# Attention bands in a written-out order on three engines, the second norm spread between two products, three sums moved to VectorE, and a strip of memory

## The chip, the cores and the metric

The kernel runs on one core of a Trainium2 chip. The metric is the device time of one execution, in microseconds (us); the kernel before took 2420.7 us (median of three). Five engines work side by side and meet through semaphores: TensorE (PE, matrix products and transposes into PSUM), VectorE (DVE), ScalarE (ACT), GpSimd (POOL) and SyncE (SP, which issues the DMAs).

## The reference

A two-layer encoder on 1024 tokens of width 1024, all in float32. Per layer: a modulated RMS norm, one input projection, three groups of attention heads side by side, a norm of each group's output, an output projection into the residual; then a second modulated RMS norm and a gated FFN of hidden width 2816.

```python
h = rms_norm(x, g_attn[l]) * (1 + sc_a) + sh_a
qa, ka, va, qb, kb, vb, qc, kc, vc = split_cols(h @ w_in[l], IN_SPLITS)
ya = neighborhood_attention(...)      # A: 4 heads, 2-D window of 8 x 16, relative bias
yb = sliding_window_attention(...)    # B: 6 heads, |i - j| <= 128, bias, sink logit
yc = axial_attention(...)             # C: 6 heads, dense, q/k norm and rotary
y = concatenate([rms_norm(ya, ga), rms_norm(yb, gb), rms_norm(yc, gc)])
x = x + gt_a * (y @ w_o[l])
h = rms_norm(x, g_ffn[l]) * (1 + sc_f) + sh_f
gate, up = split_cols(h @ w_gu[l], (FFN_HIDDEN, FFN_HIDDEN))
x = x + gt_f * ((silu(gate) * up) @ w_down[l])
```

For an A or B head only keys near the query count, so for each block of 128 queries the scores form a band of at most 384 keys.

## The kernel before

**Numbers.** Float32 operands are split into a high and a low part (`hi`, `lo`); a full product is three matmuls (`mm3`, line 202), in the attention's value product two. Splitting costs one ACT instruction (the high part) and one subtraction on DVE or POOL (the low part): `split_tile` (153) gives `whi` and `wlo` of a weight tile, `y_split` (1520) the two halves of the attention output as operand `qk`.

**Who sets the order.** Every instruction passes through the class `Engine` (37 to 61), so all rows of the profile name its line 49. A scheduler may reorder the instructions of an engine as their data allow. `pin` (92) turns that off for chosen engines: from then on each instruction is chained to the one issued before it on the same engine, so that the engine runs them in the order in which the program writes them, and one that waits holds up all behind it.

**The attention stream** (1580 to 1651). The 64 units of work are "pairs": two blocks of 128 queries of one head. Pairs 0 to 23 are C pairs (dense, 1024 keys), 24 to 39 A pairs and 40 to 63 B pairs; A and B pairs are the *bands* (class `Band`, 1384; `PairA` and `PairB` give the bias). One pass `n` of the loop at 1584 issues steps of several pairs, in two halves `i`: `turn` of pair n, `pv` of pair n-1, and `qk` of the pairs that begin, three (`AHEAD`) or, in the bands, five (`AHEAD_B`) ahead. Only POOL is pinned in this loop (1582). A band pair goes through these steps:

- `qk` (1395): four score matmuls on PE into PSUM (tiles `sA`, `sB`); per block one fused DVE instruction that adds the bias and takes the row minimum (a custom operation, tile `pr`); the exponential on ACT with its sum; then, through `unfinished`, `divide` (1149): a reciprocal on DVE and two scalings on POOL.
- `turn` (1422): four PE transposes into a PSUM tile `T`, an ACT copy to the high part and a DVE subtraction to the low part (both named `pt`); one or two further transposes of the band's edges, copied by ACT (odd pairs) or DVE (even pairs) to `edge`.
- `pv` (1450, through `products`, 1258): four matmuls and one or two of the edges (each of these shows as two in the trace) into the PSUM tile `pv`, which an even pair opens and the following odd pair fills.
- `combine` (1280), behind the odd pair: ACT copies one half of `pv` to `cmb`, DVE adds the halves into the output `y`.

PSUM holds two tiles of two banks for scores (`psS`), three for `T`, and a single one for `pv` (`psV`). The tile `T` also serves the statistics and spreadings below.

Written among the pairs are other tasks (1598 to 1650). `preload` loads the heads of later pairs. After each group of heads, `norm_sum` (1491) squares `y` on ACT, `stats` (1640) sums over partitions with 16 small matmuls (`ps_st`) and computes 1/sqrt by eleven small DVE operations (`inv_sqrt`, 427), and `norm_scale` (1502) spreads the result with four transposes (`ps_r`), an ACT copy and multiplications on POOL. At 55 and 59 `y_split` prepares the output projection, at 59 and 61 `split_tile` splits two tiles of w_o, at 61 to 64 `o_rows` (1539) does the projection's first matmuls (`ps_o`), and at 62 two more tiles of w_o are loaded and split on DVE. After the loop comes the rest of that projection.

**Gate/up** (1845 to 2020). The FFN products use seven products for eight, per column block `q`: even q is gate, odd q is up. For the first seven blocks (`EARLY`, loop at 1979) products 1 and 2 come ahead, while the rest of the normed input is still being made; `t2_part`, `t3_part` and `t4_part` make its sums on DVE and split them (`ht1` to `ht4`, `h22`). `norm` is the generator `rstd_rows` (458): its first step is the statistic, its second the spreading of the second norm with four transposes (`ps_r`), taken as `rows` at line 1990, after block 1's products and the loading of further columns. In the second loop (2002) the other products follow. `gu_product` (1847) copies a product from PSUM on ACT (`u`, `sg`), adds on DVE, and has POOL do the sum of product 7 (1886) and the products of gate and up (1869, 2009).

**Memory.** The pool `ct` (830) lives in the projections of each layer; the five lines above `bias_rows` (959), where two tiles are allocated, run in layer 0 only, and a tile that is allocated there moves the addresses of what is allocated behind it.

## Time and profile before

| what | value |
|---|---|
| median of three runs | 2420.7 us (2420.62 to 2425.7) |
| the profiled execution's own time | 2422.97 us |
| its span in the profile | 2421.1 us |
| mean granted clock of PE | 0.994 |
| PE busy | 2350.5 us, 97% |
| DVE busy | 1766.8 us, 73% |
| ACT busy | 1194.3 us, 49% |
| POOL busy | 753.4 us, 31% |

The rows of the profile name a line, an engine, an operation and its tiles, as output, an arrow, and inputs. A group ends with its busy time, the mean of one instruction in ns, and the idle time of the engine just before these instructions with what ended it. A timeline row begins with its start and its duration. Successive matmuls overlap, so their durations add up to more than the time that they take; the distance between starts is the cost.

### The profile page before, as it was taken

The page shows a single profiled execution, that of the slowest core. Times are in us where ns is not written, and L with a number is a line of the kernel's source. Part 1 is how long each engine was busy: PE and PEld are TensorE (multiplying, and loading weights), DVE is VectorE, ACT ScalarE, POOL GpSimd, SP SyncE. Part 2 cuts the span into 40 slices and gives each one's busy share as a digit, 9 for nine tenths or more (in the row PEclk, how much of TensorE's full clock was granted, in tenths as well). Part 3 has the DMA queues.
Part 4 walks back from the last instruction along what each step waited for, and adds up shares of the span by engine and source line. Part 5 has one row for each costly group of instructions (what it writes and reads, how often), then busy time and mean ns, then how long its engine had stood idle before and what let it go on. Part 6 is the DMA issues. An engine that isn't in the chain of part 4 may idle for free.

```text
span 2421.1 us, 33439 instructions
## 1 busy us (share of the span) xinstructions
PE 2350.5 (97%) x11733; PEld 1955.2 (81%) x11733; DVE 1766.8 (73%) x2782; ACT 1194.3 (49%) x2250; POOL 753.4 (31%) x725
## 2 busy tenths in 40 slices
PE   8999999999999999999999999999999999999998
PEld 5778798888787887888787879987878888888886
DVE  5756898976958888586677579988787545447865
ACT  3421788954543333344543148897454333334443
POOL 1530345610344344300036114464005444430001
PEclk9999999999999999999999999999999999999999
DMA  8478215154245454586434851142524332329643
GB/s 263 149 237 274 62 27 145 47 193 138 87 145 178 157 189 147 176 268 195 148 93 120 283 178 27 45 140 70 194 93 153 125 100 96 114 92 304 209 129 109
DMA packets 305335, 356.95 MB, mean 147 GB/s; under 512 B 51964, under 2 KB 221788, under 8 KB 305168
## 3 DMA queue, kind: packets, MB, share of 16 engines
q1 hardware_dynamic: 283296, 342.07, 44.4%
q10 hardware_dynamic: 21504, 12.59, 2.0%
q8 instruction: 92, 1.51, 0.2%
q14 instruction: 75, 0.61, 0.1%
q0 software_dynamic: 368, 0.17, 0.0%
HBM read 269.79 MB, written 88.63 MB: 148 GB/s over the span
## 4 chain that ended last, share of the span: by engine, by line
PE 48%; DVE 4%; issue 4%; DMA 2%; ACT 2%; POOL 2%; ACTq 0%; SPq 0%; POOLq 0%; DVEq 0%
PE ps_w L49 21%; PE ps_d L49 14%; PE ps_o L49 3%; PE pv L49 2%; PE T L49 2%; PE ps_v L49 2%; PE sC L49 2%; DMA qkd<-qko 1%; ACT pr L49 1%; PE ps_c L49 1%; POOL ct L49 1%; PE ps_ab L49 0%; DVE acc L49 0%; DMA graw<-gpd 0%; POOL pr L49 0%
## 5 line engine op out<-in xcount | busy, mean ns | idle before, releaser
L49 PE MATMUL ps_d<-wpt 128*128 128x512 f32 x1848 | 424.3, 390 | 2.4 <-ACT wpt L49 2.1
L49 PEld LDWEIGHTS ps_d<-wpt 128*128 128x128 f32 x1848 | 345.5, 188 | 76.4 <-issue 3.0
L49 POOL TENSOR_SCALAR pr<-pr,rs 128x1024 f32<-128x1024 f32 (+2 forms) x248 | 187.0, 768 | 227.8 <-DVE rs L49 212.8
L49 POOL TENSOR_TENSOR sg<-sg,u 128x512 f32<-128x512 f32 x86 | 125.5, 1461 | 354.5 <-ACT sg L49 117.9
L49 PE MATMUL pv<-pt,vs 128*128 128x256 f32 x1088 | 181.4, 297 | 7.3 <-ACT pt L49 2.7
L49 ACT CAST wpt<-w 128x512 fp32r<-128x512 f32 x154 | 95.7, 621 | 185.8 <-PE ps_d L49 168.0
L49 DVE TENSOR_TENSOR pt<-T,pt 128x512 fp32r<-128x512 f32 x272 | 178.5, 682 | 8.5 <-ACT pt L49 7.1
L49 PE MATMUL T<-identr,pr 128*128 128x128 f32 x1176 | 175.6, 273 | 2.6 <-ACT edge L49 0.8
L49 ACT CAST pt<-T 128x512 fp32r<-128x512 f32 x272 | 153.1, 586 | 40.5 <-PE T L49 38.1
L49 ACT COPY u<-ps_w 128x512 f32<-128x512 f32 x128 | 75.1, 586 | 192.1 <-PE ps_w L49 192.0
L49 DVE TENSOR_TENSOR wpt<-w,wpt 128x512 fp32r<-128x512 f32 x154 | 108.9, 707 | 82.1 <-ACT wpt L49 82.1
L49 POOL TENSOR_TENSOR wpt<-ws,wpt 128x512 fp32r<-128x512 f32 x80 | 111.6, 1395 | 180.8 <-ACT wpt L49 133.9
L49 PEld LDWEIGHTS pv<-pt,vs 128*128 128x128 f32 x1088 | 143.9, 189 | 21.1 <-DVE y L49 11.1
L49 PEld LDWEIGHTS T<-identr,pr 128*128 128x128 f32 x1176 | 139.9, 140 | 19.7 <-ACT edge L49 2.2
L49 DVE SCALAR_TENSOR_TENSOR acc<-wmt,condT,acc 128x512 f32<-128x512 f32 (+1 forms) x98 | 119.2, 1225 | 47.8 <-DMA wmt<-in_w_mod_dram 47.2
L49 ACT CAST wpt<-ws 128x512 fp32r<-128x512 f32 x176 | 107.8, 622 | 61.4 <-issue 26.6
L49 DVE TENSOR_TENSOR wpt<-ws,wpt 128x512 fp32r<-128x512 f32 x96 | 81.6, 861 | 60.3 <-ACT wpt L49 60.2
L49 DVE TENSOR_TENSOR wpt<-graw,wpt 128x512 fp32r<-128x512 f32 x154 | 110.0, 715 | 19.0 <-ACT wpt L49 19.0
L49 DVE TENSOR_REDUCE rs<-sC 128x1 f32<-128x1024 f32 x88 | 107.3, 1221 | 16.4 <-PE sC L49 12.4
L49 DVE TENSOR_TENSOR ws<-wr 128x512 f32<-128x512 f32 x88 | 80.0, 911 | 51.3 <-POOL wpt L49 48.1
L49 ACT CAST wpt<-graw 128x512 fp32r<-128x512 f32 x154 | 95.0, 617 | 43.3 <-DMA graw<-gpd 37.9
L49 PE MATMUL ps_w<-h22h,wpt 128*128 128x512 f32 x352 | 111.2, 397 | 4.6 <-ACT sg L49 3.6
(298 smaller groups left out, 5964.4 us busy)
## 6 DMA issues: line engine op xcount, KB each, us to landing
wr<-in_w_gu_dram SPq DMA_DIRECT2D x92, 512.0 KB, 4.1
gpd<-sg SPq DMA_DIRECT2D x154, 256.0 KB, 4.4
graw<-gpd SPq DMA_DIRECT2D x76, 512.0 KB, 3.6
w<-in_w_down_dram SPq DMA_DIRECT2D x110, 256.0 KB, 5.4
wmt<-in_w_mod_dram SPq DMA_DIRECT2D x48, 512.0 KB, 6.4
qk<-qkd SPq DMA_DIRECT2D x44, 512.0 KB, 6.8
wst<-in_w_o_dram SPq DMA_DIRECT2D x32, 512.0 KB, 3.7
wmt<-in_w_mod_dram SPq DMA_DIRECT2D x64, 256.0 KB, 3.8
```

The costliest lines, as they stand in the source:

```text
L49: ins = op(*args, **kwargs)
```

## The change

Four things change.

1. **Bands.** The methods of `Band` are cut into steps: `scores` (PE and DVE), `exps` (ACT), `divide` (DVE and POOL), `turn` (PE, the high copy and the edge copy), `low` (the DVE subtraction), `pv` (both halves), `fold` (the ACT copy `cmb`) and `combine` (the DVE addition). From pass 24 (`NC`) on PE, ACT, DVE and POOL are pinned, and one pass writes: low of n-1, addition of n-3, scores of n+4, exponentials of n+3, turn of n, pv and fold of n-2, division of n+2; then the tasks above, in their old places. `AHEAD_B` is 4, the loop runs two passes longer, and the norms' squares follow the additions, two passes later.
2. **The second norm's spreading** stands between the two early products of block 1.
3. **Three POOL operations go to DVE**: product 7's sum for blocks 0 and 1, and the product of gate and up at the head of block 1.
4. **A strip** of 192 bytes a partition is allocated in layer 0's `ct`.

```diff
--- before.py
+++ after.py
@@ -955,6 +955,7 @@
             sp.dma_start(mB, C["maskB"])
             dve.tensor_copy(t5h[:, 0, :], t5)
             dve.tensor_tensor(out=t5h[:, 1, :], in0=t5, in1=f32(t5h[:, 0, :]), op=ALU.subtract)
+            pad(ct, 48)
 
         def bias_rows():
 
@@ -1274,18 +1275,24 @@
                             stop=(n == len(movs) - 1 and i == len(mvs) - 1),
                             skip_group_check=True,
                         )
-                if part and self.p % 2:
-                    self.combine()
-
-            def combine(self):
-
+
+            def fold(self):
+
+                if self.p % 2 == 0:
+                    return
                 r0 = (self.row % 2) * 64
                 o0 = 64 - r0
+                self.t = atp.tile([P, H], F32, name="cmb", tag="cmb", bufs=1)
+                act.copy(self.t[r0 : r0 + 64], self.pvt[o0 : o0 + 64])
+
+            def combine(self):
+
+                if self.p % 2 == 0:
+                    return
+                r0 = (self.row % 2) * 64
                 half = self.p // 2
-                t = atp.tile([P, H], F32, name="cmb", tag="cmb", bufs=1)
-                act.copy(t[r0 : r0 + 64], self.pvt[o0 : o0 + 64])
                 to = y[r0 : r0 + 64, self.row // 2, :]
-                a, b = self.pvt[r0 : r0 + 64], t[r0 : r0 + 64]
+                a, b = self.pvt[r0 : r0 + 64], self.t[r0 : r0 + 64]
                 if self.by_columns:
                     to = to.rearrange("p (r j i) -> p j r i", j=8, i=8)
                     to = to[:, half * 4 : half * 4 + 4]
@@ -1343,6 +1350,9 @@
                     ],
                     part,
                 )
+                if part:
+                    self.fold()
+                    self.combine()
 
         def load_q(dst, oc, j):
             sp.dma_start(f32(dst), qkd[oc, j].rearrange("z p t -> (z p) t"))
@@ -1392,62 +1402,60 @@
                 self.pr = self.flat[:, 0:770].rearrange("p (c k) -> p c k", c=2)
                 self.spans = [(0 if p > 0 else P, 384), (0, 384 if p < 3 else 256)]
 
-            def qk(self, c):
+            def scores(self):
                 rs, p, sk = self.rs, self.p, self.sk
-                if c == 0:
-                    self.s = psS.tile([P, 2, 512], F32, name=self.name, tag="S")
-                s, pr = self.s, self.pr
-                j = 2 * p + c
-                a, b = self.spans[c]
-                for i in range(2):
-                    pe.matmul(
-                        s[:, c, a:b], self.q[:, j * P : (j + 1) * P],
-                        self.k[i][:, (j - 1) * P + a : (j - 1) * P + b],
-                        start=(i == 0), stop=(i == 1),
+                s, pr = psS.tile([P, 2, 512], F32, name=self.name, tag="S"), self.pr
+                for c, (a, b) in enumerate(self.spans):
+                    j = 2 * p + c
+                    for i in range(2):
+                        pe.matmul(
+                            s[:, c, a:b], self.q[:, j * P : (j + 1) * P],
+                            self.k[i][:, (j - 1) * P + a : (j - 1) * P + b],
+                            start=(i == 0), stop=(i == 1),
+                        )
+                    sv, pw, z = s[:, c, a:b], pr[:, c, a:b], self.bias(j, a, b)
+                    if z.ndim > 2:
+                        sv, pw = (t.rearrange("p (b k) -> p b k", k=P) for t in (sv, pw))
+                    dve.tensor_tensor_reduce(
+                        out=pw, in0=sv, in1=z, scale=1.0, scalar=BIG if sk is None else sk,
+                        op0=ALU.add, op1=ALU.min, accum_out=rs[:, c : c + 1],
                     )
-                sv, pw, z = s[:, c, a:b], pr[:, c, a:b], self.bias(j, a, b)
-                if z.ndim > 2:
-                    sv, pw = (t.rearrange("p (b k) -> p b k", k=P) for t in (sv, pw))
-                dve.tensor_tensor_reduce(
-                    out=pw, in0=sv, in1=z, scale=1.0, scalar=BIG if sk is None else sk,
-                    op0=ALU.add, op1=ALU.min, accum_out=rs[:, c : c + 1],
+
+            def exps(self):
+                for c, (a, b) in enumerate(self.spans):
+                    e = self.pr[:, c, a : b + (self.sk is not None)]
+                    act.activation(
+                        e, e, AF.Exp, bias=self.rs[:, c : c + 1], scale=-1.0,
+                        accum_out=self.rs[:, 2 + c : 3 + c],
+                    )
+
+            def divide(self):
+                divide([self.pr[:, c, a:b] for c, (a, b) in enumerate(self.spans)], self.rs)
+
+            def turn(self):
+                pr = self.pr
+                T, self.pt = t_tile(), [pt_tile() for _ in range(2)]
+                for b in range(2):
+                    for i in range(2):
+                        pe.transpose(
+                            T[:, 2 * b + i, :], pr[:, b, (1 - b + i) * P : (2 - b + i) * P], ident
+                        )
+                edges = [pr[:, 0, 0:P]] * self.left + [pr[:, 1, 2 * P : 3 * P]] * self.right
+                E = t_tile()
+                for i, src in enumerate(edges):
+                    pe.transpose(E[:, i, :], src, ident)
+                hi, lo = (
+                    t[:, 0:2, :].rearrange("p i (c q) -> p c i q", c=2) for t in self.pt
                 )
-                e = pr[:, c, a : b + (sk is not None)]
-                act.activation(
-                    e, e, AF.Exp, bias=rs[:, c : c + 1], scale=-1.0,
-                    accum_out=rs[:, 2 + c : 3 + c],
+                T = T.rearrange("p (c i) q -> p c i q", c=2)
+                act.copy(hi, T)
+                e = self.e = atp.tile([P, 2, P], F32, name="edge", tag="edge", bufs=3)
+                (act.copy if self.p % 2 else dve.tensor_copy)(
+                    e[:, 0 : len(edges)], E[:, 0 : len(edges)]
                 )
-                self.finish(pr[:, c, a:b])
-
...
+                self.low = lambda: sub(lo, T, f32(hi))
+
+            def pv(self):
                 k0, e = 2 * self.p, self.e
                 movs = [
                     (k0 + i, slice(0, 2 * P), [t[:, i, :] for t in self.pt]) for i in range(2)
@@ -1456,7 +1464,8 @@
                     movs.append((k0 - 1, slice(0, P), [e[:, 0]]))
                 if self.right:
                     movs.append((k0 + 2, slice(P, 2 * P), [e[:, int(self.left)]]))
-                self.products(movs, part)
+                for part in range(2):
+                    self.products(movs, part)
 
 
         class PairA(Band):
@@ -1578,22 +1587,52 @@
         later = {}
         N = len(stream)
         pairs = {}
-        AHEAD, AHEAD_B = 3, 5
+        AHEAD, AHEAD_B, NC = 3, 4, 24
         pin((pool,), True)
         made, done = 0, len(first_pairs)
-        for n in range(-AHEAD - 1, N + 1):
-            ahead = AHEAD if n + AHEAD < 24 else AHEAD_B
+        scored, worked = [], []
+        for n in range(-AHEAD - 1, N + 3):
+            ahead = AHEAD if n + AHEAD < NC else AHEAD_B
             begin = range(done, min(n + ahead + 1, N))
-            for i in range(2):
-                if 0 <= n < N:
-                    pairs[n].turn(i)
-                while unfinished:
-                    unfinished.pop(0)()
-                if 0 <= n - 1 < N:
-                    pairs[n - 1].pv(i)
-                for m in begin:
-                    if m < made:
-                        pairs[m].qk(i)
+            if n == NC:
+                pin((pe, act, dve), True)
+            if n < NC:
+                for i in range(2):
+                    if 0 <= n:
+                        pairs[n].turn(i)
+                    while unfinished:
+                        unfinished.pop(0)()
+                    if 0 <= n - 1:
+                        pairs[n - 1].pv(i)
+                    for m in begin:
+                        if m < min(made, NC):
+                            pairs[m].qk(i)
+                fresh = [pairs[m] for m in begin if NC <= m < made]
+                for b in fresh:
+                    b.scores()
+                    b.exps()
+                    b.divide()
+            else:
+                if NC <= n - 1 < N:
+                    pairs[n - 1].low()
+                if NC <= n - 3:
+                    pairs[n - 3].combine()
+                fresh = [pairs[m] for m in begin if m < made]
+                for b in fresh:
+                    b.scores()
+                for b in scored:
+                    b.exps()
+                if n < N:
+                    pairs[n].turn()
+                if NC <= n - 2 < N:
+                    pairs[n - 2].pv()
+                    pairs[n - 2].fold()
+                elif n == NC:
+                    for i in range(2):
+                        pairs[n - 1].pv(i)
+                for b in worked:
+                    b.divide()
+                scored, worked = fresh, scored
             done = max(done, min(begin.stop, made))
             while made < min(N, n + ahead + 2):
                 for key, make in preload.get(made, []):
@@ -1623,9 +1662,9 @@
                 o_rows(1, w01[1], range(NS)[2 * (n - 63) : 2 * (n - 62)])
             if n == 62:
                 wq = [w_rows(w_o, k * P, eng=dve) for k in korder[2:4]]
-            m = n - 1
+            m = n - 1 if n <= NC else n - 3
             for end, (chunks, width) in norms.items():
-                if begins[end] <= m <= end and (m - begins[end]) % 8 == 7:
+                if begins[end] <= m <= end and (m - begins[end]) % 8 == 7 and (n <= NC or m >= NC):
                     i = (m - begins[end]) // 8
                     if end not in gss:
                         gss[end] = gss_tile()
@@ -1648,7 +1687,7 @@
                             later.setdefault(n + 8, []).append(scale)
 
                         later.setdefault(n + 5, []).append(stats)
-        pin((pool,), False)
+        pin((pe, act, dve, pool), False)
         close(psV_cm)
         close(psT_cm)
         close(vs_cm)
@@ -1883,7 +1922,7 @@
             elif num == 7:
                 take("x")
                 t22 = t["22"]
-                pool.tensor_tensor(out=t22, in0=t22, in1=t["x"], op=ALU.add)
+                (pool if q > 1 else dve).tensor_tensor(out=t22, in0=t22, in1=t["x"], op=ALU.add)
                 done(o[:, hi], t["22"], pool)
             elif num == 3:
                 add("12")
@@ -1980,14 +2019,14 @@
             for i in range(2):
                 a = [w[:, 4 * i : 4 * i + 4] for w in early[q]]
                 gu_product(q, PRODUCTS[i], a)
+                if q == 1 and i == 0:
+                    rows = next(norm)
             if q + 4 < EARLY:
                 early.append(first_cols((q + 4) % 2 * FF + (q + 4) // 2 * 2 * P))
             elif raw0 is None:
                 raw0 = gu_raw(0)
             if q == 0:
                 next(norm)
-            if q == 1:
-                rows = next(norm)
             if 1 <= q < 5:
                 bs.append(t2_part(q - 1, rows))
             if q == 1:
@@ -2006,7 +2045,9 @@
                 up = q % 2
                 e = sg[q // 2][0][:, 0:H]
                 if up:
-                    pool.tensor_tensor(out=e, in0=e, in1=quads[q]["11"], op=ALU.mult)
+                    (pool if q > 1 else dve).tensor_tensor(
+                        out=e, in0=e, in1=quads[q]["11"], op=ALU.mult
+                    )
             for i, p in enumerate(PRODUCTS[2 if q < EARLY else 0 :]):
                 gu_product(q, p, ahead.get())
                 if i == 1 and q < EARLY and not up:
```

More of the change, by code (lines that the diff above doesn't have):

```diff
@@ L1422, in turn @@
-            def turn(self, c):
-                pr = self.pr
-                T = t_tile()
-                if c == 0:
-                    self.pt = [pt_tile() for _ in range(2)]
-                    for b in range(2):
-                        for i in range(2):
-                            pe.transpose(
-                                T[:, 2 * b + i, :], pr[:, b, (1 - b + i) * P : (2 - b + i) * P],
-                                ident,
-                            )
-                    hv, lv = (
-                        t[:, 0:2, :].rearrange("p i (c q) -> p c i q", c=2) for t in self.pt
-                    )
-                    split_pt(T.rearrange("p (c i) q -> p c i q", c=2), hv, lv)
-                    return
-                e = self.e = atp.tile([P, 2, P], F32, name="edge", tag="edge", bufs=3)
-                n = 0
-                for left, here in ((True, self.left), (False, self.right)):
-                    if here:
-                        src = pr[:, 0, 0:P] if left else pr[:, 1, 2 * P : 3 * P]
-                        pe.transpose(T[:, n, :], src, ident)
-                        n += 1
-                if self.p % 2:
-                    act.copy(e[:, 0:n], T[:, 0:n])
-                else:
-                    dve.tensor_copy(e[:, 0:n], T[:, 0:n])
@@ L1450, in pv @@
-            def pv(self, part):
+                s, pr = psS.tile([P, 2, 512], F32, name=self.name, tag="S"), self.pr
[13 more added lines that the diff above has]
+                        op0=ALU.add, op1=ALU.min, accum_out=rs[:, c : c + 1],
+                    )
```

1 line of the change is left out of this document (removed).

## The prediction

> **What bounds the kernel now.** The page's first part comes first: TensorE (PE) is busy for nearly the whole span, so time moves only where PE is idle, slow or given other work.
>
> ```profile
> span 2421.1 us, 33439 instructions
> PE 2350.5 (97%) x11733; PEld 1955.2 (81%) x11733; DVE 1766.8 (73%) x2782; ACT 1194.3 (49%) x2250; POOL 753.4 (31%) x725
> ```
>
> A busy share can hide pipelined matmuls, so I next asked for the stretches that the change touches: the bands of layer 0 (from the first transpose of pair 24 to the last matmul of pair 63), the same of layer 1, two parts of layer 0's bands (split at the first transposes of pairs 28 and 57), gate/up of layer 0, and a short piece of that. Columns: bounds and length, busy time of each engine (count), granted clock, DMA share, GB/s.
>
> ```profile
> core 0: us, PE busy (x) PEld busy (x) DVE busy (x) ACT busy (x) POOL busy (x), PEclk, DMA share, GB/s
> 389.90:498.20 108.30, 103.19 (x733) 90.26 (x731) 97.91 (x292) 96.13 (x248) 66.73 (x117) 1.00 0.36 103
> 1570.50:1678.85 108.35, 103.36 (x734) 90.49 (x733) 98.18 (x292) 96.22 (x248) 66.93 (x118) 1.00 0.36 103
> 398.23:475.87 77.64, 74.43 (x535) 65.16 (x534) 69.05 (x228) 71.22 (x194) 52.29 (x95) 1.00 0.36 104
> 475.87:498.46 22.59, 20.69 (x135) 17.33 (x134) 21.51 (x41) 17.43 (x36) 8.95 (x13) 1.00 0.23 75
> 596.00:640.00 44.00, 40.42 (x170) 32.27 (x169) 43.72 (x64) 23.20 (x39) 5.11 (x3) 0.96 0.22 72
> 636.50:640.00 3.50, 3.46 (x9) 2.79 (x10) 3.38 (x5) 1.25 (x2) 1.71 (x1) 0.58 0.87 293
> ```
>
> In the bands three engines are near full at once: VectorE (DVE) 90%, ScalarE (ACT) 89%, PE 95%. No single one sets the pace; their order does. In gate/up DVE is full (43.72 of 44.00), PE waits for it, and at 636.5 PE's clock fell to 0.58.
>
> The groups of the bands (busy, mean ns, idle before) and a short timeline give what one pair costs.
>
> ```profile
> L49 PE MATMUL T<-identr,pr 128*128 128x128 f32 x220 | 37.7, 274 | 1.3 <-ACT edge L49 0.4 <-DVE edge L49 0.3 <-DVE pt L49 0.2
> L49 PE MATMUL pv<-pt,vs 128*128 128x256 f32 x176 | 34.2, 306 | 1.7 <-DVE y L49 0.8 <-DVE pt L49 0.5
> L49 DVE TENSOR_TENSOR pt<-T,pt 128x512 fp32r<-128x512 f32 x42 | 28.8, 687 | 1.3 <-ACT pt L49 0.8
> L49 ACT CAST pt<-T 128x512 fp32r<-128x512 f32 x41 | 23.9, 584 | 3.4 <-PE T L49 3.0
> L49 ACT ACTIVATE pr<-pr,rs 128x385 f32<-128x385 f32 x36 | 22.1, 615 | 0.6 <-POOL pr L49 0.4
> L49 PE MATMUL pv<-edge,vs 128*128 128x128 f32 x120 | 20.2, 274 | 0.0
> L49 DVE TENSOR_TENSOR y<-pv,cmb 64x512 f32<-64x512 f32 x20 | 13.7, 686 | 1.5 <-ACT cmb L49 1.1
> L49 ACT COPY cmb<-pv 64x512 f32<-64x512 f32 x20 | 11.6, 581 | 2.5 <-PE pv L49 2.1
> L49 DVE TENSOR_TENSOR wlo<-wst,whi 128x1024 fp32r<-128x1024 f32 x5 | 6.8, 1369 | 0.3 <-ACT whi L49 0.2
> L49 ACT CAST whi<-wst 128x1024 fp32r<-128x1024 f32 x5 | 5.2, 1048 | 0.7 <-DMA wst<-in_w_o_dram 0.7
> L49 ACT ACTIVATE gsq<-y 128x512 f32<-128x512 f32 x7 | 4.4, 635 | 0.6 <-DVE y L49 0.6
> L49 ACT ACTIVATE qk<-y,vecs 128x512 fp32r<-128x512 f32 x5 | 3.6, 726 | 0.0
> ```
>
> ```profile
> 440.25 0.52 PE L49 MATMUL pv<-pt,vs 128*128 128x256 f32 x3
> 442.56 0.60 PE L49 MATMUL T<-identr,pr 128*128 128x128 f32 x4
> 442.93 0.98 PE L49 MATMUL sB<-qk 128*128 128x384 f32 x4
> 443.97 1.84 PE L49 MATMUL ps_st<-onesr,gss 128*128 128x1 f32 x16
> ```
>
> ```profile
> 442.25 0.62 DVE L49 CUSTOM_DVE_ANT_0 pr<-sB,bz,sinkc 128x384 f32<-128x384 f32 x1
> 442.79 0.68 DVE L49 TENSOR_TENSOR pt<-T,pt 128x512 fp32r<-128x512 f32 x1
> 444.65 0.68 DVE L49 TENSOR_TENSOR y<-pv,cmb 64x512 f32<-64x512 f32 x1 [0.33 <-ACT cmb L49]
> ```
>
> Back to back, an instruction costs less than its duration. Four transposes last 0.60 and one 0.27, so they start (0.60-0.27)/3 = 0.11 apart; by the same reckoning a pv matmul of 256 columns costs 0.12, a score matmul of 384 columns about 0.18, and a transpose-sized edge matmul 0.11. On DVE the score step at 442.25 is followed 0.54 later, against its 0.62. One band pair on PE is thus: scores about 0.65, on average 5.5 transposes 0.60, pv 4 x 0.12 + 3 x 0.11 = 0.80; sum **2.05 us**. DVE, with the same overlap: two score steps 1.08, the low half 0.61, half a y addition 0.3, and some 0.15 for the small rest; sum about 2.1. ACT: two exponentials 1.2, the high half 0.50, half a cmb copy 0.25, the rest 0.15; sum about 2.1. The middle part now takes 77.64/29 = 2.68 us a pair, extras included.
>
> **The change, part by part.**
>
> *Bands, steady pace.* Nothing is computed less; the order is fixed and the steps stand further apart. A new limit is the one pv bank (psV). Between the pv of an odd pair and of the next even one stand the cmb copy (0.58) on ACT, the y addition (0.69) on DVE, the matmul's tail (about 0.16) and handoffs of about 0.04 each (three): 1.55. PE has the next scores and transposes for that time: 0.65 + 0.60 = 1.25. So 0.30 is lost each second pair, 0.15 a pair. For the passing to and fro between PE's three T banks and the copies I add 0.07: 2.05 + 0.15 + 0.07 = **2.27 us**, an estimate; its bounds are 2.05 (PE alone) and today's 2.68.
>
> *What is now nailed into that order.* Four kinds of work stood free before, and the engines could pass them; now all behind them wait. Each statistics step (pairs 29 and 47) is 16 small matmuls, 16 x 0.11 = 1.8 on PE, and DVE's chain of eleven small operations waits for them, with the next low half, y addition and score steps queued behind; I take 3.0 (bounds 1.8, PE's part alone, and 3.2, with two waiting DVE operations of 0.69). Each spreading (32, 50): four transposes 0.44 and ACT's copy ahead of its exponentials; I take 1.2 (0.44 to 1.5). The split of y at 55: ACT 0.73, then DVE about 0.7 (half of a wlo, which is twice as wide), and behind it the addition of pair 53 for which the pv of pair 54 waits; with handoffs I take 1.9 (bounds 0 and 2.3). Middle part: 29 x 2.27 + 2 x 3.0 + 2 x 1.2 + 1.9 = 76.1 against 77.64: **-1.5**.
>
> *The end of the bands.* At 59 a y split and a w_o split are written between the fold of pair 57 and its addition. After pv 57 ends there follow, in order: cmb 0.58, square 0.63, y 0.73, whi 1.05 (ACT), wlo 1.37, low half 0.69, addition 0.69 (DVE): 5.7, with handoffs 5.9; PE has only the transposes of pair 60 (0.60). I take 4.9 of idle time before pv 58, since the square may come earlier. At 61 the same without square and y: 0.58 + 1.05 + 1.37 + 0.69 + 0.69 = 4.4, with handoffs 4.7, against 0.60 of transposes and six output matmuls of 0.23 (1.4): 2.7; I take 2.3. At 62 two further weight rows are split, and their load stands between:
>
> ```profile
> wst<-in_w_o_dram SPq DMA_DIRECT2D x32, 512.0 KB, 3.7
> 594.97 0.39 PE L49 MATMUL ps_w<-h21l,whi 128*128 128x512 f32 x1
> 595.20 0.60 PE L49 MATMUL ps_r<-identr,rstd 128*128 128x128 f32 x4
> ```
>
> (The second and third rows also give a 512-column matmul: 0.23.) The load's 3.7 less the 2.0 that PE has meanwhile (transposes 0.60, output matmuls 1.4) leaves 1.7; I take 1.8 (0 to 3.7) before pv 62, whose opening waits for the addition of pair 61 behind that split. SyncE's queue stays unpinned, and the loads keep their place in the program. PE's work from transpose 57 to pv 63: 2 scores 1.3, 7 turns 4.2, 9 pv 7.2, 24 output matmuls 5.4: 18.1. With 4.9 + 2.3 + 1.8 it is 27.1 against 22.59 now: **+4.5** (bounds 18.1 and 29).
>
> *The start of the bands.* Pairs 24 to 27 run into the pinned order over pv 23, a dense one: I take +0.6 on the 8.33 us (398.23 less 389.90) to pair 28 (0 to +1.0). The scores of pair 28 move behind the first transposes: 0.65 earlier there, 0.65 later here, nothing in sum. POOL was pinned before; its two scalings per pair and the sink copies only move with the division, which stands two pairs (4.5 us) ahead of its transposes, and POOL is busy 66.73 of 108.30, 1.7 a pair: I cost this at nothing, and at up to 0.3 a pair if that lead is gone. The squares for the norms move two turns later with the additions that they read; they are the same instructions.
>
> *Clock.* PE's clock is the second price of an idle spell:
>
> ```profile
> 636.54 1.22 PE L49 MATMUL ps_w<-h22h,wpt 128*128 128x512 f32 x2 [1.80 <-ACT sg L49]
> 1298.62 0.50 PE L49 MATMUL ps_ab<-hh,wlo 128*128 128x512 f32 x1 [1.66 <-POOL wlo L49]
> 1298.70:1302.00 3.30, 3.30 (x15) 2.73 (x16) 3.27 (x6) 0.43 (x1) 3.22 (x4) 1.00 0.51 159
> ```
>
> After 1.80 idle the clock was 0.58 for 3.5 us; after 1.66 it stayed 1.00. So three of the new gaps (4.9, 2.3, 1.8) lie where a slow spell may come. One costs up to 3.5 x 0.42 = 1.5; as PE has slack here I take **+1.9** for the three (0 to 4.5). For T banks handed out in turn, where a slow reader holds up a free one, I take **+0.5** (0 to 3.8, one T copy of 0.58 for each of six to seven held turns).
>
> Bands, sum: 0.6 - 1.5 + 4.5 + 1.9 + 0.5 = **+6.0 a layer, +12.0**.
>
> By the Trainium skill, "TensorE: Matmul & The Clock Gate", section "What's actually happening", the clock halves after at least one idle window of some 3.4 us. By that rule only the 4.9 gap pays; the trace disagrees as far as it goes (1.80 was enough once), and I weigh it as a rival.
>
> *Gate/up.*
>
> ```profile
> 595.47 0.69 DVE L49 TENSOR_TENSOR u<-u,ps_w 128x512 f32<-128x512 f32 x1 [4.29 <-PE ps_w L49]
> 629.35 0.73 PE L49 MATMUL ps_w<-ht3h,wpt 128*128 128x512 f32 x2 [0.81 <-ACT sg L49]
> 633.32 0.73 PE L49 MATMUL ps_w<-ht4h,wpt 128*128 128x512 f32 x2 [0.96 <-ACT u L49]
> 631.79 1.77 DVE L49 TENSOR_TENSOR ht4l<-xb,ht4h 128x512 fp32r<-128x512 f32 x1
> 635.19 0.68 DVE L49 TENSOR_TENSOR ht4l<-xb,ht4h 128x512 fp32r<-128x512 f32 x1
> 631.32 3.40 POOL L49 TENSOR_TENSOR sg<-sg,u 128x512 f32<-128x512 f32 x2 [114.15 <-DMA wr<-in_w_gu_dram]
> ```
>
> DVE stands idle for 4.29 us before its full stretch, because the four spreading transposes (595.20) come after both products. Between the products they come 12 x 0.23 = 2.7 earlier. How much of it DVE gets depends on whether the addition of the second product, which ends where it did, stays ahead of the first norm operation: 0.5 if so, 2.7 if not. Three sums on DVE add 3 x 0.61 = 1.8; but while POOL did two of them, DVE's ht4l took 1.77 against 0.68 undisturbed, about 1.0 more for each sum: net -1.2. So DVE arrives 1.7 to 3.9 earlier where PE now waits 0.81 + 0.96 + 1.80 = 3.57, and with less than 1.8 idle the slow spell (1.5) can go. I take the middle for the waits and two fifths of the spell: 2.8 + 0.6 = **-3.4 a layer** (-1.0 to -5.1), **-6.8** in all.
>
> *The strip* has no instruction; it moves addresses in layer 0. No row shows an address at work: 0, bounds -2 and +2 (about the 1.66 us wait seen in that kind of stage).
>
> **Sum.** +12.0 - 6.8 = +5.2 on the profiled execution's own 2422.97 us (span 2421.1) is 2428.2. That execution lies 2.27 above the median of three, 2420.7; on the median the forecast is **2425.9 us**.
>
> **The rivals.**
>
> *Faster: the splits hide.* If ACT runs a pair ahead of PE, whi and y are done before pv 57 ends, and the end chain is only cmb, low half and addition (2.0 against 0.6 of turns). Then the end loses half of today's 4.5: 18.1 + 2.3 = 20.4 (-2.2), the split at 55 nothing (middle -3.4), no slow clock: 0.6 - 3.4 - 2.2 + 0.2 = -4.8 a layer; with gate/up 2420.7 - 9.6 - 6.8 = **2404.3**. For it: ACT is 11% idle. Against: its 2.1 a pair nearly equals the pace, so it gains no lead. It decides from about 3 us of ACT lead at pair 57.
>
> *Much slower: more slow clock, held T banks.* Four spells at 1.4 (the gap before pv 54 included) and 1.4 for banks in place of 1.9 and 0.5: 3.6 + 5.6 + 1.4 = 10.6 a layer; 2420.7 + 21.2 - 6.8 = **2435.1**. For it: 1.80 us sufficed at 636.54. Against: 1.66 did not at 1298.62.
>
> *No change: short gaps leave the clock alone.* Only the gap of 4.9 slows it (0.6): 3.6 + 0.6 + 0.5 = 4.7 a layer; +9.4 - 6.8 gives **2423.3**. The 1298.62 row speaks for it. That is also what the page's rule would give.
>
> **How the numbers follow.** About 0.2% (4.8 us) is what can be told from no change. The forecast (chance 0.45; 2413 to 2433) splits into 0.07 faster, 0.14 same, 0.24 slower. The faster rival has 0.20, all faster; the much slower one 0.17, all slower; the third 0.18: 0.04 faster, 0.12 same, 0.02 slower. Sums: faster 0.31, same 0.26, slower 0.43. The range runs from 2406 (half of the faster rival left out) to 2437 (half of the much slower one): 2 in 10 outside. It covers the bounds of the tail (18.1 to 29) and of the clock taken singly.
>
> **What would show it.** Bands of a layer over 112 us, with PE idle over 4 us once near pv 58 and over 1.5 us about twice more, each ended by the y addition; transposes 28 to 57 about 76 us. In gate/up: DVE's first norm operation near 593 rather than 596, ht4l under 1 us, and the gap at 636.54 gone or below 1 us. The forecast is wrong if the bands come in under 106 us, if the end shows no y addition late, or if the PE clock in the bands stays 1.00 throughout.

## The result

The changed kernel takes 2548.9 us (median of four, 2547.1 to 2553.5) against 2421.6 for the kernel before (median of four; three of these runs gave the 2420.7 that the forecast started from), a ratio of 1.0525 (95% interval 1.0506 to 1.0544). The forecast was 2425.9 with a range of 2406 to 2437. The sign was right, the size wrong by a factor of about 25 (127 us for 5.2).

The page of the changed kernel, its first two lines and one group that was far down the list before (busy, mean ns, idle before it and what ended that); the last row is the same kind of matmul for the A pairs, from the list of PE's groups:

```profile
span 2551.8 us, 33458 instructions
PE 2376.6 (93%) x11733; PEld 1979.9 (78%) x11733; DVE 1771.6 (69%) x2788; ACT 1197.5 (47%) x2250; POOL 742.9 (29%) x719
L49 PE MATMUL sB<-qk 128*128 128x384 f32 (+1 forms) x192 | 59.3, 392 | 68.7 <-DVE rs L49 65.5
L49 PE MATMUL sA<-qk 128*128 128x384 f32 (+1 forms) x128 | 38.8, 392 | 34.2 <-DVE rs L49 30.8 <-ACT pr L49 3.4
```

PE runs the same 11733 instructions. Of the 131 us that the span is longer, PE is idle for 105; for 26 it is busier, with a slower clock. Of its idle time 68.7 us stand ahead of one kind of matmul, the score matmuls of the B pairs, and nearly all of that ends with `rs`, the row minimum that a score step on VectorE writes. The A pairs add 34.2, so that `rs` ends 96.3 us in all. The stretches of the changed kernel that answer to those of before: the bands of layer 0, their middle part (transposes of pair 28 to 57), their end, gate/up, and a piece of the end.

```profile
396.13:567.70 171.57, 114.27 (x737) 100.39 (x736) 101.58 (x290) 97.61 (x249) 64.59 (x114) 0.91 0.25 70
411.63:534.81 123.18, 81.53 (x528) 71.71 (x527) 74.40 (x229) 70.00 (x187) 50.64 (x92) 0.90 0.22 61
534.81:567.70 32.89, 23.16 (x142) 20.38 (x141) 18.24 (x35) 17.92 (x36) 8.18 (x14) 0.90 0.21 65
660.00:704.00 44.00, 43.27 (x193) 35.50 (x192) 41.99 (x64) 24.67 (x40) 1.35 (x1) 1.00 0.23 72
549.02:552.80 3.78, 3.77 (x18) 3.78 (x19) 0.79 (x4) 0.84 (x2) 3.41 (x5) 0.50 0.32 122
```

The bands of layer 0 take 171.6 us in place of 108.3 (here to the end of the last matmul; below, the length of the bands goes to its start, which is 0.3 earlier). In the middle 123.18/29 is 4.2 us a pair, against 2.68 before and 2.27 forecast. DVE and ACT, nine tenths busy before, are at 60%: no engine is the bound, the order is. Gate/up keeps a clock of 1.00 where it had 0.96, and PE is busy for 43.27 us where it had 40.42.

The timeline of PE over one pass in the middle (start, duration, operation, idle time before it):

```profile
475.58 0.62 PE L49 MATMUL sB<-qk 128*128 128x384 f32 x2 [1.60 <-DVE rs L49]
476.04 0.71 PE L49 MATMUL T<-identr,pr 128*128 128x128 f32 x5
476.50 0.72 PE L49 MATMUL pv<-pt,vs 128*128 128x256 f32 x4
477.06 0.60 PE L49 MATMUL pv<-edge,vs 128*128 128x128 f32 x4
477.42 0.60 PE L49 MATMUL sB<-qk 128*128 128x384 f32 x2
478.74 0.62 PE L49 MATMUL sB<-qk 128*128 128x384 f32 x2 [0.72 <-DVE rs L49]
```

and of DVE in the same time:

```profile
474.44 0.68 DVE L49 TENSOR_TENSOR y<-pv,cmb 64x512 f32<-64x512 f32 x1 [0.39 <-ACT cmb L49]
475.05 0.47 DVE L49 CUSTOM_DVE_ANT_0 pr<-sB,bz,sinkc 128x256 f32<-128x256 f32 x1
478.06 0.62 DVE L49 CUSTOM_DVE_ANT_0 pr<-sB,bz,sinkc 128x384 f32<-128x384 f32 x1
479.50 0.62 DVE L49 CUSTOM_DVE_ANT_0 pr<-sB,bz,sinkc 128x384 f32<-128x384 f32 x1 [0.82 <-PE sB L49]
```

The four score matmuls of a pair do not run together. Two for block 0 start at 477.42; the two for block 1 start at 478.74, just after DVE's step on block 0 (478.06, 0.62 long) has ended; and DVE's step on block 1 then waits for them until 479.50. Where the low half and the y addition stand ahead of DVE's first step, the pause is 1.60 instead of 0.72. It is a chain PE, DVE, PE, DVE in every pass, and since PE is pinned, transposes and pv stand behind it.

### The profile page after: what moved, and what is told of

Same layout as the page of the kernel before. It is cut to its first block, busy times and chain, and to the rows that moved or that the text cites. A ratio compares the mean times of both kernels' runs of the same rounds, so it can differ in the third digit from the quotient of the medians.

```text
span 2551.8 us, 33458 instructions
## 1 busy us (share of the span) xinstructions
PE 2376.6 (93%) x11733; PEld 1979.9 (78%) x11733; DVE 1771.6 (69%) x2788; ACT 1197.5 (47%) x2250; POOL 742.9 (29%) x719
## 5 line engine op out<-in xcount | busy, mean ns | idle before, releaser
L49 POOL TENSOR_TENSOR sg<-sg,u 128x512 f32<-128x512 f32 x82 | 116.7, 1424 | 354.3 <-ACT sg L49 227.7
L49 DVE TENSOR_TENSOR pt<-T,pt 128x512 fp32r<-128x512 f32 x272 | 178.1, 682 | 18.1 <-ACT pt L49 16.4
L49 PE MATMUL T<-identr,pr 128*128 128x128 f32 x1176 | 169.3, 282 | 0.0
L49 PEld LDWEIGHTS T<-identr,pr 128*128 128x128 f32 x1176 | 146.0, 146 | 14.1
L49 PE MATMUL sB<-qk 128*128 128x384 f32 (+1 forms) x192 | 59.3, 392 | 68.7 <-DVE rs L49 65.5
L49 DVE TENSOR_TENSOR wlo<-wst,whi 128x1024 fp32r<-128x1024 f32 x66 | 81.6, 1237 | 51.2 <-ACT whi L49 48.3
```

Source lines behind the costliest of these rows:

```text
L49: ins = op(*args, **kwargs)
```

## The experiments

The theory after the result: both blocks of a pair lie in one PSUM tile, and in the program the first block's DVE step, which reads that tile, stands ahead of the second block's matmuls, which write into it; so they wait for it, though they touch another bank. The rivals: the waits that the prediction did name (the single pv bank with its late y addition, the tasks nailed into the order, the slow clock) are simply larger; or the order of the steps is to blame and not the tile.

**e1_matmuls_first**

```diff
                 for c, (a, b) in enumerate(self.spans):
                     j = 2 * p + c
                     for i in range(2):
                         pe.matmul(s[:, c, a:b], ...)
+                for c, (a, b) in enumerate(self.spans):
+                    j = 2 * p + c
                     sv, pw, z = s[:, c, a:b], pr[:, c, a:b], self.bias(j, a, b)
```

> The changed kernel, but in the step scores all four matmuls of a pair are written ahead of the two VectorE score steps. Theory: the 66 us that each layer's bands lost come from the second block's matmuls waiting for the first block's VectorE step, because both blocks lie in one PSUM tile; then the bands fall from 171 to about 113 us a layer (the pace of 2.27 us and the end of the prediction), the kernel to 2424 us, 2415 to 2436. Rival: the single pv bank with the late y addition, and the slow clock, make the loss; then the bands stay above 160 us and the kernel above 2530 us.

2457.6 us (ratio 1.0133, 1.0113 to 1.0153): 91 us come back. The bands fall to 127.5 and 127.2 us. No idle time ahead of an sB matmul with `rs` as its cause is left. But this lies above the 2424 of the theory: a second cause is worth 19 us a layer; e5 shows it.

**e2_tile_per_block**

```diff
-                s, pr = psS.tile([P, 2, 512], F32, name=self.name, tag="S"), self.pr
+                pr = self.pr
                 for c, (a, b) in enumerate(self.spans):
+                    s = psS.tile([P, 2, 512], F32, name=self.name, tag="S")
```

> The changed kernel with its written order as it is (matmuls of block 0, VectorE step 0, matmuls of block 1, VectorE step 1), but each block has a PSUM tile of its own from the same two slots. Theory, the wait comes from the shared tile and not from the order: block 1 waits only for the step of a block of the pair before, and the kernel comes to 2424 to 2445 us. Rival, the wait belongs to the order of the steps: it stays near 2549 us.

2461.5 us (1.0157, 1.0140 to 1.0174). The steps stand in the order that the change wrote, yet 87 us are back. So it is the shared tile, not the order of these steps. The view of the tile sB lists the idle time ahead of its instructions by cause (us, times); these are the rows for `rs` in the kernel before, in the changed kernel, and in e2:

```profile
  DVE rs L49: 7.7, 23
```

```profile
  DVE rs L49: 148.7, 94
```

```profile
  DVE rs L49: 5.2, 20
```

(The view adds the waits of matmuls and of weight loads, so one pause on PE appears twice.) 94 times is thus some 47 pauses, about one for each of the 48 B pairs of the two layers; the matmuls' share is the 65.5 us of the page.

**e12_tensor_free**

```diff
-                pin((pe, act, dve), True)
+                pin((act, dve), True)
```

> The changed kernel with its shared tile, ScalarE and VectorE pinned from pair 24 on, TensorE not. Theory: what costs is that TensorE's queue stands behind the second block's matmuls; with TensorE free most of the 45 us a layer come back: 2440 to 2480 us. Rival: VectorE's fixed order holds the loop as well, since its second score step waits for the same matmuls: above 2520 us.

2495.6 us (1.0298, 1.0277 to 1.0320), bands 151.1 and 152.1 us. Neither side's number came out. Of the 127 us, 53 come back with PE alone free: its idle time ahead of the score matmuls that ends with `rs` falls from 96.3 to 18.2 us. But DVE's score steps still wait for their matmuls in a fixed queue (in the view of sB 45.6 us in 54 places in the changed kernel, and here):

```profile
  PE sB L49: 35.7, 28
```

How the 71 us that remain over the kernel before (2424.4 beside it) divide between this wait and the tasks nailed into the order of DVE and ACT is not shown; no run frees these two one by one.

**e7_no_pins**

```diff
-            if n == NC:
-                pin((pe, act, dve), True)
```

> The changed kernel with its steps and its shared tile as they are, but TensorE, ScalarE and VectorE are not pinned (only GpSimd, as before). Theory: the wait between the two blocks of a pair costs 45 us a layer only because nothing else may go ahead of the waiting matmul; with free order it is filled: 2415 to 2435 us. Rival: the wait costs in any order: above 2480 us.

2419.9 us (0.9979, 0.9965 to 0.9993). With the shared tile and all the steps of the change, but a free order, the bands take 111.4 us. The wait is still there (8.8 us in 13 places in the view of sB), but other work goes ahead meanwhile (eight transposes at 442.27, between score matmuls at 441.81 and 443.51), and PE's idle time ahead of the score matmuls that ends with `rs` is 4.0 us, not 96.3. With e9 below the comparison is complete: in a free order the shared tile costs 2.5 us a layer (111.4 against 108.9), in the pinned one 44 to 47 (the changed kernel against e1).

**e5_extras_free**

```diff
+            if n >= NC:
+                pin((pe, act, dve), False)
             for what in later.pop(n, []):
...
+            if n >= NC:
+                pin((pe, act, dve), True)
             m = n - 1 if n <= NC else n - 3
```

> The kernel of e1 (2457.6 us), in which the tasks between the pairs (statistics, spreading, splits, first output matmuls) are not pinned to the written order on TensorE, ScalarE and VectorE; the steps of the pairs stay pinned. Theory: what e1 still loses against the kernel before, 19 us a layer, is these tasks nailed into the order: statistics and spreading 7.5 and 4.1 us, the split at 55 3.9 us, the end 8.5 us above the pace; at least half of the 24 us goes, so 2410 to 2434 us. Rival: the pace of the pairs itself (2.4 us against 2.27) and the slow clock make it; then it stays above 2450 us.

2417.2 us (0.9960, 0.9947 to 0.9973). e1 against e5, first e1, then e5, bands, middle and end:

```profile
392.63:520.40 127.77, 105.51 (x736) 97.47 (x736) 99.39 (x299) 97.37 (x254) 65.36 (x115) 0.93 0.34 95
402.07:489.32 87.25, 73.11 (x528) 68.25 (x527) 70.80 (x230) 71.25 (x194) 52.36 (x95) 0.94 0.33 90
489.32:520.40 31.08, 23.33 (x141) 20.90 (x140) 19.78 (x38) 17.65 (x36) 8.89 (x14) 0.88 0.22 69
```

```profile
385.02:495.00 109.98, 99.04 (x737) 91.51 (x737) 95.89 (x299) 96.87 (x253) 67.78 (x115) 1.00 0.39 110
394.47:471.55 77.08, 68.83 (x528) 64.56 (x527) 68.51 (x230) 71.42 (x193) 51.54 (x93) 1.00 0.37 102
471.55:495.00 23.45, 21.12 (x142) 18.62 (x141) 18.40 (x39) 17.00 (x36) 12.21 (x17) 1.00 0.30 91
```

17.8 us of the 19 are the tasks between the pairs: 10.2 in the middle, 7.6 at the end, and with them the slow clock goes (1.00). DVE in e1 at the second statistics shows how one of them costs more than was priced (rows are left out between these):

```profile
455.14 0.16 DVE L49 RECIPROCAL rs<-rs 128x2 f32<-128x2 f32 x1
456.67 0.17 DVE L49 TENSOR_SCALAR isq<-ps_st 128x8 f32<-128x8 f32 x1 [1.37 <-PE ps_st L49]
457.96 0.17 DVE L49 SCALAR_TENSOR_TENSOR isq<-isq 128x8 f32<-128x8 f32 x1
458.16 0.17 DVE L49 SCALAR_TENSOR_TENSOR rstd<-isq,rstd 128x8 f32<-128x8 f32 x1
459.36 0.17 DVE L49 SCALAR_TENSOR_TENSOR rstd<-isq,rstd 128x8 f32<-128x8 f32 x1
460.15 0.69 DVE L49 TENSOR_TENSOR y<-pv,cmb 64x512 f32<-64x512 f32 x1
```

Each of the eleven small operations needs the one before it, and in this chain they start 0.20 apart (457.96, 458.16); an operation that does not need the one ahead of it can follow after 0.07 (448.92 and 448.99 in the kernel before). From 455.3 to 459.4 DVE does nothing for the pairs: it waits until 456.67 for the statistic, then come the chain and, among it, a split of y (0.75). So pv comes 3.03 us late for its y addition.

**e10_norms_free**: as e5, but the pins return ahead of the splits and output matmuls.

```diff
+            if n >= NC:
+                pin((pe, act, dve), False)
             for what in later.pop(n, []):
                 what()
+            if n >= NC:
+                pin((pe, act, dve), True)
```

> The kernel of e1 in which only the norms' tasks (squares, statistics, spreading) are not pinned; the splits and the output matmuls stay in the written order. From the trace of e5 against e1, the statistics and spreadings give back 6.3 and 2.0 us a layer: 2457.6 - 17 = 2441 us (2435 to 2447). Rival: it was the splits at the end that held everything: 2450 us or more.

2436.0 us (1.0053, 1.0033 to 1.0073), bands 119.5: the norms' tasks alone give 8 of the 17.8 us a layer, the splits the rest. The gap ahead of pv 58 stays, here 5.33 us.

**e6_two_pv_banks**

```diff
-PS_T = 3
+PS_T = 2
```

> The kernel of e1 with two PSUM banks for pv and two, not three, for the transposes. Theory: in e1 every second pair loses 0.6 to 0.8 us to the one pv bank (matmuls waiting for the y addition); with a second one the pace falls from 2.4 to 2.06 us a pair, some 9 us a layer: 2440 us. Rival: with two tiles for transposes, which also hold the edges, these wait for the low half of the pair before, and it gets slower than 2458 us.

2477.7 us (1.0205, 1.0178 to 1.0232), bands 131.2 and 129.9. The groups of layer 0's bands in e1, then in e6:

```profile
L49 PE MATMUL pv<-pt,vs 128*128 128x256 f32 x176 | 33.4, 317 | 21.8 <-DVE y L49 18.6 <-ACT qk L49 3.0
L49 PE MATMUL T<-identr,pr 128*128 128x128 f32 x220 | 32.6, 282 | 0.4 <-DVE pt L49 0.2 <-DVE edge L49 0.2
```

```profile
L49 PE MATMUL T<-identr,pr 128*128 128x128 f32 x220 | 37.8, 293 | 21.2 <-DVE pt L49 16.6 <-DVE rs L49 4.2
L49 PE MATMUL pv<-pt,vs 128*128 128x256 f32 x176 | 33.1, 316 | 0.0
```

The wait for the y addition goes, 21.8 to 0.0, and comes back ahead of the transposes, 0.4 to 21.2. The bank was the named limit, but behind it DVE's queue stands in both cases. The rest of the loss lies in the dense C pairs, which use the same banks: from layer 0's first transpose to its bands 142.6 us pass, against 136.1 in e1.

**e3_gate_up_alone** (parts 2 and 3 of the change on the kernel before), **e11_spreading_alone** (part 2), **e4_strip_alone** (part 4):

```diff
+                if q == 1 and i == 0:
+                    rows = next(norm)
...
-            if q == 1:
-                rows = next(norm)
...
```

(e3 also has the three operations of the change on DVE, e4 only the line `pad(ct, 48)`.)

> The kernel before with the gate/up part of the change alone (the spreading between the products, three sums on VectorE). By the prediction -6.8 us, so 2415 us; by the trace of the changed kernel, whose gate/up stretch is 3.8 us shorter in each layer, 2414 us. Rival: what gate/up gains is given back in the down projection of layer 0, which is 3 us longer there: 2417 us.

> The kernel before with the spreading between the two products alone, the three sums left on GpSimd. By the prediction VectorE's full stretch starts up to 2.7 us earlier, but the sums on GpSimd still slow VectorE by about 1 us each: of the 8 us of e3 some 4 to 5 come, 2418 to 2420 us. Rival: the spreading brings all of it, 2415 us; or nothing, 2423 us.

> The kernel before with the strip alone. By the prediction no change, within 2 us of the kernel before. Rival: moved addresses cost the 3 us by which the down projection of layer 0 is longer in the changed kernel: +3 us.

e3: 2414.7 us against 2422.6 (0.9965, 0.9952 to 0.9977), -8.5 by the ratio. e11: 2416.7 against 2424.4 (0.9979, 0.9967 to 0.9990), -5.1 by the ratio. e4: 2425.1 against 2422.6 (1.0005, 0.9994 to 1.0016): nothing that can be told from no change. The other stages shift by 2 or 3 us from execution to execution (the down projection of layer 0 too), so the rival that it gives back gate/up's gain is not borne out: its 2417 us lie at the edge of e3's interval, and in e3 the down projection of layer 0 takes 214.4 us, against 214.6 in the kernel before, 217.6 in the changed one and 215.4 in e4; layer 0's bands repeat within 0.1 us in before, e3 and e4.

**e8_gate_up_and_matmuls_first** and **e9_no_pins_matmuls_first**: the lesson of e1 on the kernel before, with e3's gate/up, and on e7.

```diff
             def qk(self, c):
...
+                if c == 0:
+                    for d, (a, b) in enumerate(self.spans):
+                        j = 2 * p + d
+                        for i in range(2):
+                            pe.matmul(s[:, d, a:b], ...)
...
-                for i in range(2):
-                    pe.matmul(s[:, c, a:b], ...)
```

> The kernel before with the gate/up part (2414.7 us in e3) and with both blocks' score matmuls of a band pair ahead of the first VectorE step. In the trace of before TensorE's weight loads idle 3.2 us a layer ahead of sB matmuls for this wait. Theory: that goes, -3 to -6 us, 2409 to 2412 us. Rival: the first VectorE step now waits for both blocks, and nothing is won: 2414 us or more.

> The kernel of e7 (changed, TensorE, ScalarE and VectorE not pinned) with all score matmuls of a pair first, as in e1. Theory: with free order the wait between the blocks is mostly filled, and taking it away is worth as little as in e8, 0 to 4 us: 2414 to 2420 us on the scale where the kernel before has 2424. Rival: with fewer waits the steps reach their pace of 2.06 to 2.3 us a pair: below 2410 us.

e8: 2414.3 us (0.9947, 0.9931 to 0.9962), bands 106.8 in both layers against 108.3; 12.9 us faster than before by the ratio, the lowest ratio here. By the ratios it is 4.4 us under e3, but the two intervals overlap; what the traces show is 1.5 a layer in the bands, 3.0 in all, the lower end of the expected 3 to 6. e9: 2415.7 us (0.9967, 0.9954 to 0.9980), bands 108.9 against 111.4 in e7.

## Why the prediction was wrong

**The step that failed** is the steady pace, and in it a wait that was put at nothing. "One band pair on PE is thus: scores about 0.65" counted four matmuls back to back; in the changed kernel the second block's two start 1.32 after the first's (477.42 and 478.74), and a pair takes 4.2 us, not 2.27. The row that was quoted for it, four sB matmuls at 442.93, holds blocks of different pairs, which wait for nothing of each other; in the kernel before, a pair's blocks stood in different halves of a pass. The diff put them into one loop with the DVE step between, and the prediction did not ask what the second block's matmuls wait for. It listed a wait for the pv bank and not this one. Worth 44 and 47 us a layer (bands 171.2 and 174.4 in the changed kernel, 127.5 and 127.2 in e1), it is three quarters of the loss. That PE and its weight loads idled for the same `rs` ahead of sB in the kernel before was in its trace (7.7 us in 23 places, above); there it cost little.

With that wait gone (e1), the other terms can be measured, layer 0 each:

| term | forecast | e1 |
|---|---|---|
| transposes of 24 to 28, with pair 28's scores | 9.6 | 9.4 |
| pace in the middle, us a pair (e1: pairs 34 to 45) | 2.27 | 2.44 |
| middle | 76.1 | 87.3 |
| idle before pv 58 | 4.9 | 5.68 |
| idle before pv 60 | 2.3 | 1.97 |
| idle before pv 62 | 1.8 | 0.0 |
| end | 27.1 | 30.8 |

The two gaps, in the timeline of e1:

```profile
501.71 1.20 PE L49 MATMUL pv<-pt,vs 128*128 128x256 f32 x4 [5.68 <-DVE y L49]
510.58 0.59 PE L49 MATMUL pv<-pt,vs 128*128 128x256 f32 x3 [1.97 <-DVE y L49]
```

**The end** was right in mechanism for the first two gaps (5.04 and 2.22 in the changed kernel). The third did not come: PE had output matmuls to do until 517.1, where pv 62 starts. PE's own work was set too low, at 18.1: it is busy for 23.33 in e1, with a clock of 0.88, and for 21.12 in e5 at 1.00. **The middle** was too low by 11 us: the pace by 0.17 a pair (5 us), the statistics and spreadings by 3.5 (11.9 above the pace in pairs 28 to 33 and 46 to 51, where 8.4 was taken, and the small operations at 0.20 each are seen in it), the split at 55 by 2 (4.0 for 1.9). These are distances between first transposes in the timeline, the slow clock included.

**The clock.** The granted clock (PEclk, the third number from the end) stands at 0.50 three times in layer 0's bands of e1, at the gaps of 3.03, 2.97 and 5.68:

```profile
458.96:465.78 6.82, 4.88 (x21) 4.78 (x22) 4.94 (x18) 1.83 (x6) 1.35 (x4) 0.50 0.00 0
486.26:489.68 3.42, 3.42 (x14) 3.32 (x15) 1.87 (x8) 1.20 (x4) 1.28 (x3) 0.50 0.00 0
499.92:506.74 6.82, 5.03 (x22) 4.96 (x23) 2.57 (x7) 1.76 (x5) 3.39 (x5) 0.50 0.24 77
```

PE is busy for 13.3 us of them, half of which, 6.7 us, is lost (an estimate), against 1.9 taken for three spells. After the gaps of 1.97 and 1.99 in e1 the clock stayed at 1.00, after one of 2.00 in e2 it fell. In the changed kernel the piece from 549.02 has 0.50. So the forecast was right that gaps well under 3.4 us can slow the clock and wrong to give each of some 2 us an equal weight. The rule of the Trainium skill ("TensorE: Matmul & The Clock Gate", section "What's actually happening"), an idle window of some 3.4 us, does not agree with these gaps: 2.97 was enough, and 2.00 in e2.

What separates them in these traces is where a gap lies. In each trace of this case the granted clock changes only at points that are whole multiples of 3.41 us apart, and every spell at 0.50 between two such changes lasts 3.41, 6.83 or 10.24 us. Cut at these points, the stretch with the gap of 2.00 in e2 and the one behind it, then the same around the gap of 1.97 in e1:

```profile
409.50:412.91 3.41, 1.41 (x11) 1.18 (x10) 3.24 (x13) 1.24 (x4) 0.00 (x0) 1.00 0.01 5
412.91:416.32 3.41, 3.41 (x18) 3.41 (x17) 2.38 (x9) 1.42 (x5) 2.20 (x4) 0.50 0.34 106
```

```profile
506.74:510.15 3.41, 1.87 (x12) 1.37 (x10) 2.13 (x3) 2.72 (x4) 0.00 (x0) 1.00 0.00 0
510.15:513.57 3.42, 2.99 (x20) 2.71 (x21) 1.75 (x3) 0.77 (x1) 0.00 (x0) 1.00 0.71 192
```

The gap in e2 lies whole in one stretch, and PE is busy for 1.41 us of it; the one in e1 is cut in two, and 1.87 busy kept the clock. Two more fit: 1.80 in the kernel before shares its stretch, from 632.64, with a part of the 0.96 ahead of it (1.42 busy, then 0.50), and one of 2.86 in e10 left the clock at 1.00, cut in two at 473.82 (1.93 and 2.03 busy). Busy time is not the whole rule: ahead of the spell at 458.96 in e1 PE was busy for 2.33 of 3.41, ahead of one at 449.93 in e10 for 3.23, and in both stretches many one-column matmuls of a statistic stand.

**The rivals.** "Much slower" named the clock and the T banks; the clock's price in e1, 6.7 a layer, is near its 5.6, and PE idled 0.4 us ahead of the transposes, but neither made the loss of the changed kernel. "No change" had the gaps near 2 us right in e1, but not the two near 3. "The splits hide" fell: they cost their 7.6 us at the end. All three, like the forecast, took over its pace.

**Gate/up** held: -3.4 a layer forecast, -8.5 by e3's ratio for both, -3.9 a layer in the traces, from the first early product's first matmul to the first with h22 (53.2 us before, 49.3 in the changed kernel). In the changed kernel DVE starts its norms after 1.89 idle, not 4.29, and PE's three gaps of 3.57 shrink to one of 0.73:

```profile
661.78 1.40 DVE L49 SCALAR_TENSOR_TENSOR xb<-xb,gsc,ps_r 128x512 f32<-128x512 f32 x2 [1.89 <-PE ps_r L49]
```

```profile
700.58 0.73 PE L49 MATMUL ps_w<-ht4h,wpt 128*128 128x512 f32 x2 [0.73 <-ACT u L49]
```

The addition of the second product does not hold it up. The sums on DVE bring the rest, 3.4 us by the two ratios, whose intervals overlap; in the trace of e11 DVE still needs 3.47 for two ht4l and PE still waits 1.60:

```profile
632.89 3.47 DVE L49 TENSOR_TENSOR ht4l<-xb,ht4h 128x512 fp32r<-128x512 f32 x2
```

```profile
637.03 0.73 PE L49 MATMUL ps_w<-h22h,wpt 128*128 128x512 f32 x2 [1.60 <-ACT sg L49]
```

**The strip**: nothing, as forecast.

**Is a written order worth something here?** In e5, where only the pairs' own steps are pinned, the bands take 109.6 us; free in e9, 108.9; the old steps in e8, 106.8. None of the runs shows a gain from it. The new steps in a free order do have the shortest middle (74.0 us in e9; 75.2 in e8, 77.1 in e5, 77.6 before), but the longest end of these four (26.5).

## What to carry to other kernels

When an order is written out and pinned, go through each engine's list and ask of every instruction what it waits for in the new neighbourhood, dependences by tile and not only by data included: a wait that a free queue passes at no cost becomes the pace when nothing may pass it. A price taken from matmuls that stand side by side in a trace holds only if they stand beside each other for the same reason in the new order. And write producers for both halves of a shared tile before the first reader.

## What had not been expected of the hardware

Small dependent DVE operations of 8 elements start 0.20 us apart when nothing stands between them. PE's granted clock changes on a fixed grid of 3.41 us in each trace, so that a gap of 2.00 us inside one stretch halved it (1.41 busy) and one of 2.86 across two did not (1.93 and 2.03 busy). Where the limit lies, and how matmuls of different size count towards it, stays open, since no run varied a gap by itself.
